# A rotary half swap done by VectorE products that write to other partitions, in place of SBUF-to-SBUF DMAs

## The chip, the cores and the metric

The kernel runs on one core of a Trainium2 chip. Its engines run their own instruction queues side by side and meet through semaphores: TensorE (PE in the profile; its weight loads are PEld), VectorE (DVE), ScalarE (ACT), GpSimd (POOL) and SyncE (SP). DMAs are issued from the queues of SP, ACT and POOL. The metric is the time of one execution on the device in microseconds, as the median of several runs.

## What is computed

The reference is a decoder trunk with two layers on 512 tokens of width 1024. Each layer adds the output of three token mixers that share one input projection (MLA attention with 4 heads, gated linear attention "GLA" with 4 heads, retention with 4 heads), and then the output of a convolutional gated MLP. The change concerns the rotary embedding, which the MLA queries, the one MLA key shared by all heads, and the retention queries and keys go through:

```python
def apply_rope(x, cos, sin):
    half = x.shape[-1] // 2
    c = cos[None, :, None, :].astype(x.dtype)
    s = sin[None, :, None, :].astype(x.dtype)
    x1, x2 = x[..., :half], x[..., half:]
    return jnp.concatenate([x1 * c - x2 * s, x2 * c + x1 * s], axis=-1)
...
q_nope, q_rope = q[..., :MLA_NOPE], apply_rope(q[..., MLA_NOPE:], cos, sin)
k_r = apply_rope(k_rope[:, :, None, :], cos, sin)[:, :, 0, :]
...
qh = apply_rope(q.reshape(B, S, RET_HEADS, RET_DK), cos, sin)
kh = apply_rope(k.reshape(B, S, RET_HEADS, RET_DK), cos, sin) * (RET_DK ** -0.5)
```

## The kernel before

Activations are kept with features on the 128 partitions and the 512 tokens along the free dimension. So the two halves of a rotary vector are two blocks of partitions: for the MLA key rows 0 to 31 and 32 to 63, for a pair of MLA query heads the same twice on 128 rows, for retention rows 0 to 63 and 64 to 127 (its weight columns are packed in that order).

Each large product is made of three matmuls (`mm3`): both operands are split into a high and a low part of type fp32r by `halves` or `split` (a cast and a subtraction), and high times high, high times low and low times high are summed in PSUM. Weights arrive by SP as `raw` (three buffers), are split into `whi` and `wlo`, and in the mixers the low part is finished by an accumulating DMA on POOL's queue. All accumulation tiles share eight PSUM banks, under the tags `g` (projections), `s` (scores, transposes) and `o` (outputs of attention).

Nothing is issued as it is written. A `Recorder` collects every instruction with its reads and writes, and `schedule` plans the whole program by list scheduling with its own costs and due times; `issue` then emits that order, in which each engine works strictly. In the planner's costs a DMA from ACT takes 0.1 us to issue, then its bytes at 200 KB per us and 2.0 us (`DMA_ISSUE`, `DMA_RATE`, `DMA_LATENCY`, lines 251 to 253). An instruction with more than one form (`copy`, `scale`) goes to the engine, ACT or DVE, that the planner finds free; `tt` has the one form, on DVE. Since all are emitted by one line of `issue`, the profile shows that line (L491) for almost everything, and rows are told apart by tile names: `z0` and the results of `scaled` are `t` or `w`, the rotary tables lie in `const_rope`, `qe` and `big` belong to the scores of GLA and retention.

One layer's mixer runs in this order of the program: projection `t0` (which holds the MLA key `z0` and the gate's input), `gq0`, `gk0`, the gate of GLA (`gla_gate`: a small matmul, three ScalarE functions, a running sum by four scans), `rq0` and `rk0` with their rotary, `gla_scores` (transposes of the decayed key `kh` early on TensorE, then seven levels with masks), `ret_scores`, the values, latents and gates, the MLA key's rotary `kz`, the linear outputs, the MLA up-projections with the rotary of two query pairs, four heads of `mla_head` (scores, mask, row maximum, exponent, transposes, product with the values), and the output projection, which is accumulated in halves: the part over the linear mixers can run early and fills TensorE between the heads' first blocks. Then comes the MLP (`ffn`).

A rotary in the kernel before: ACT's queue issues one DMA for each half block (two for the key and for retention, four for a query pair), each of which copies a half of `z` to the other half's rows in `zs`; DVE multiplies `z` by the cosine, then `zs` by the signed sine, and adds. The key's result is copied to rows 64 to 127 by one more DMA, and split on 128 rows. That is 15 DMAs a layer.

Of the kernel before, what the change touches and what calls it, by code (L numbers as in the profile page):

```python
# [18 lines left out]
F32 = mybir.dt.float32  # L19
F32R = mybir.dt.float32r  # L20
I32 = mybir.dt.int32
AF = mybir.ActivationFunctionType
ALU = mybir.AluOpType
# [3 lines left out]
S = 512  # L27
# [103 lines left out]
def constants():  # L131

    first, rope, rest = Stream(), Stream(), Stream()
    i = np.arange(P)
    first.add("one", np.ones((P, 1)))
    first.add("hm", (i[:, None] // 32 == np.arange(H)[None, :]))
    first.add("ident", np.eye(P))
    first.add("ones", np.ones((P, P)))

    first.add("bias", np.where(i[None, :] <= i[:, None], 0.0, MASK_BIAS))  # L140

    t = np.arange(S, dtype=np.float32)
    for name, dim, half in (("m", 64, 32), ("r", 32, 64)):
        inv = (np.float32(10000.0) ** (-(np.arange(0, dim, 2, dtype=np.float32) / np.float32(dim)))).astype(np.float32)
        ang = (t[None, :] * inv[:, None]).astype(np.float32).astype(np.float64)
        f = i % (dim // 2)
        sign = np.where(i % (2 * half) < half, -1.0, 1.0)
        rope.add("cos" + name, np.cos(ang)[f])
        rope.add("sin" + name, np.sin(ang)[f] * sign[:, None])
    gam = 1.0 - 2.0 ** (-5.0 - np.arange(H))  # L150
    diff = i[None, :] - i[:, None]
    dt = np.stack([np.where(diff >= 0, g ** np.maximum(diff, 0), 0.0) for g in gam], axis=1)
    rest.add("rdec", dt.reshape(P, H * P))
    gp = gam[RET_ROWS // 32]
    rest.add("qdec", gp[:, None] ** (i[None, :] + 1.0))
    rest.add("kdec", gp[:, None] ** (P - 1.0 - i[None, :]))
    rest.add("cdec", (gp ** P)[:, None])
    rest.add("bd", (i[:, None] // 32 == np.arange(256)[None, :] // 64))
    rest.add("bdr", (RET_ROWS[:, None] // 32 == np.arange(256)[None, :] // 64))
    rest.add("hmr", (RET_ROWS[:, None] // 32 == np.arange(H)[None, :]))  # L160
    for s in LEVELS:
        half = s // 2
        m = np.arange(64) // half
        rest.add(f"lm{s}", (i[:, None] >= m[None, :] * s) & (i[:, None] < m[None, :] * s + half))
    return {"first": first, "rope": rope, "rest": rest}


# [336 lines left out]
class Builder:  # L504
# [208 lines left out]
    def rope(self, z, half, rows, name, out):  # L713

        nc = self.nc
        zs, t1 = self.w(), self.w()
        for p in range(0, rows, 2 * half):
            nc.scalar.dma_start(out=zs[p:p + half], in_=z[p + half:p + 2 * half], bytes_=half * S * 4)
            nc.scalar.dma_start(out=zs[p + half:p + 2 * half], in_=z[p:p + half], bytes_=half * S * 4)
        self.tt(t1[:rows], z[:rows], self.c("cos" + name)[:rows], ALU.mult)  # L720
        self.tt(zs[:rows], zs[:rows], self.c("sin" + name)[:rows], ALU.mult)
        self.tt(out[:rows], zs[:rows], t1[:rows], ALU.add)
        return out

# [40 lines left out]
    def mix(self):  # L765
        nc = self.nc
# [24 lines left out]
        for name, sc in (("rq0", 1.0), ("rk0", DK_SCALE)):  # L791
            z = self.w()
# [38 lines left out]


        kz = self.rope(z0, 32, 64, "m", self.w())
        nc.scalar.dma_start(out=kz[64:128], in_=kz[0:64], bytes_=64 * S * 4)
        kr = self.halves(kz)

        sg = self.big(NB)
        for n, ps in enumerate(tokens("g")):
# [27 lines left out]
        for u, kinds in enumerate((("n", 0, "r", 0), ("n", 1, "n", 2), ("r", 1, "n", 3))):  # L866
            wt = self.wload(f"uq{u}")
            for j in range(2):
                kind, i = kinds[2 * j:2 * j + 2]
                ps = self.ps("g")  # L870
                self.gemm(ps, wt, j * 384, cq)
                z = self.w()
# [3 lines left out]
                else:  # L876
                    z = self.rope(z, 32, P, "m", self.w())
                    for h, (own, other) in enumerate(((slice(0, 64), slice(64, P)), (slice(64, P), slice(0, 64)))):
                        x = qr[2 * i + h] = self.t(F32R)
# [333 lines left out]
```

## Time and profile before

| | |
|---|---|
| median of 3 runs | 1230.01 us (1228.95 to 1232.84) |
| the profiled execution | 1230.06 us, of it 1228.1 us from first to last instruction |
| busy, share of the span | PE 97%, PEld 81%, DVE 70%, ACT 29%, POOL 4% |
| mean granted TensorE clock | 0.989 of full |

"Busy" of PE is the time in which at least one matmul is under way; matmuls overlap, and one of 512 columns starts about every 0.23 us at full clock. Rows of the timeline give the start and length of an instruction (or of several merged ones, with their count), and in brackets how long the engine stood idle before it and what released it. In the stages by time, the two mixers are 0 to 217.6 us and 617.3 to 819.4 us, and the MLPs follow them.

### The profile page before, as it was taken

The numbers are of one execution on the slowest core, as the hardware profiler recorded it, in microseconds if no ns is written. First come the engines' busy times: TensorE is split into PE (matmuls) and PEld (weight loads), VectorE is DVE, ScalarE is ACT, GpSimd is POOL, SyncE is SP. The second block draws the span as 40 slices with busy tenths as digits, with TensorE's granted clock in tenths as the row PEclk, the third lists the DMA queues.
The fourth block names the chain that finished last, engine by engine and source line by source line (L and its number), as shares of the span: only waits on it lengthen the run. The fifth ranks groups of instructions, "written<-read, shape, count | busy, mean of one in ns | idle before, by whom it ended". The sixth has DMA issues, their size and how long they took to land.

```text
span 1228.1 us, 14686 instructions
## 1 busy us (share of the span) xinstructions
PE 1188.4 (97%) x5700; PEld 993.4 (81%) x5700; DVE 865.0 (70%) x1461; ACT 360.8 (29%) x610; POOL 51.7 (4%) x63
## 2 busy tenths in 40 slices
PE   7899989999999999999998999899999999999996
PEld 5687878888888888888886788788888888888896
DVE  7699788677654666467758988776766557654775
ACT  5354636331110111012334556442311002100232
POOL 1011110100000000000011111000000000000000
PEclk9899999999999999999998999999999999999999
DMA  8765561733332333332486654617332333333322
GB/s 280 180 144 135 137 144 38 154 121 89 101 103 87 102 100 90 103 96 72 112 194 155 152 133 104 150 26 184 99 103 87 103 97 92 103 94 95 100 72 70
DMA packets 43174, 141.24 MB, mean 115 GB/s; under 512 B 4960, under 2 KB 7392, under 8 KB 42976
## 3 DMA queue, kind: packets, MB, share of 16 engines
q1 hardware_dynamic: 32848, 107.53, 28.7%
q0 software_dynamic: 8496, 30.15, 13.3%
q10 hardware_dynamic: 1760, 2.62, 0.8%
q8 instruction: 45, 0.74, 0.3%
q14 instruction: 25, 0.20, 0.0%
HBM read 105.42 MB, written 2.10 MB: 88 GB/s over the span
## 4 chain that ended last, share of the span: by engine, by line
PE 84%; DVE 8%; DMA 4%; ACT 1%; issue 1%; ACTq 1%; SPq 0%; DVEq 0%
PE g L491 57%; PE s L491 24%; DVE w L491 3%; DMA w<-w 3%; PE o L491 3%; DVE qe L491 2%; DVE big L491 1%; DVE t L491 1%; DMA w<-t 1%; ACTq L491 1%; DMA X<-x_in 0%; ACT w L491 0%; ACT whi L491 0%; SPq L491 0%; DVE sm L491 0%
## 5 line engine op out<-in xcount | busy, mean ns | idle before, releaser
L491 PE MATMUL g<-t,whi 128*128 128x512 f32 x2088 | 650.7, 392 | 6.5 <-ACT whi L491 6.2
L491 PEld LDWEIGHTS g<-t,whi 128*128 128x128 f32 x2088 | 391.7, 189 | 87.8 <-ACT whi L491 6.9
L491 PE MATMUL g<-t,wlo 128*128 128x512 f32 x1044 | 408.5, 392 | 0.0
L491 DVE CAST whi<-raw 128x1024 fp32r<-128x1024 f32 (+2 forms) x146 | 99.8, 684 | 236.3 <-PE g L491 130.4
L491 PEld LDWEIGHTS g<-t,wlo 128*128 128x128 f32 x1044 | 197.0, 189 | 40.2 <-DVE wlo L491 0.5
L491 PE MATMUL s<-t,whi 128*128 128x512 f32 x608 | 187.1, 389 | 0.0
L491 DVE TENSOR_TENSOR wlo<-raw,whi 128x1024 fp32r<-128x1024 f32 (+2 forms) x133 | 157.6, 1185 | 2.1 <-ACT whi L491 2.1
L491 ACT ACTIVATE w<-w,par 128x512 f32<-128x512 f32 x44 | 36.0, 817 | 371.1 <-DVE w L491 371.0
L491 PEld LDWEIGHTS s<-t,whi 128*128 128x128 f32 x608 | 114.2, 188 | 23.6
L491 PE MATMUL s<-t,wlo 128*128 128x512 f32 x304 | 118.3, 389 | 0.0
L491 PE MATMUL g<-whi,t 128*128 128x512 f32 x288 | 94.7, 404 | 0.0
L491 POOL DMA_DIRECT2D wlo<-raw x59 | 51.5, 873 | 790.2 <-ACT wlo L491 629.8
L491 PE MATMUL s<-t 128*128 128x256 f32 (+2 forms) x484 | 73.3, 305 | 6.1 <-DVE t L491 6.1
L491 PEld LDWEIGHTS s<-t 128*128 128x128 f32 x484 | 64.9, 195 | 8.5 <-DVE t L491 6.9
L491 ACT ACTIVATE w<-w 128x512 f32<-128x512 f32 (+1 forms) x82 | 44.6, 558 | 88.5 <-DVE w L491 88.0
L491 DVE SCALAR_TENSOR_TENSOR w<-w,par 128x511 f32<-128x511 f32 x88 | 65.8, 748 | 1.4
L491 PEld LDWEIGHTS s<-t,wlo 128*128 128x128 f32 x304 | 57.1, 188 | 11.9
L491 PEld LDWEIGHTS g<-whi,t 128*128 128x128 f32 x288 | 55.7, 195 | 11.8 <-issue 0.8
L491 ACT CAST whi<-raw 128x1024 fp32r<-128x1024 f32 (+2 forms) x46 | 46.0, 1000 | 63.7 <-PE g L491 39.1
L491 ACT CAST t<-w 128x512 fp32r<-128x512 f32 (+1 forms) x51 | 31.6, 620 | 104.9 <-DVE w L491 96.6
L491 ACT ACTIVATE wlo<-whi 128x1024 fp32r<-128x1024 f32 (+1 forms) x45 | 46.8, 1041 | 44.5 <-PE g L491 21.7
L491 PE MATMUL g<-wlo,t 128*128 128x512 f32 x144 | 58.1, 404 | 0.0
(120 smaller groups left out, 1038.5 us busy)
## 6 DMA issues: line engine op xcount, KB each, us to landing
raw<-w_l SPq DMA_DIRECT2D x174, 512.0 KB, 3.5
wlo<-raw POOLq DMA_DIRECT2D x53, 512.0 KB, 4.9
raw<-w_l SPq DMA_DIRECT2D x22, 384.0 KB, 3.2
wlo<-raw POOLq DMA_DIRECT2D x6, 384.0 KB, 4.0
X<-x_in SPq DMA_DIRECT2D x8, 256.0 KB, 6.0
out<-w SPq DMA_DIRECT2D x8, 256.0 KB, 2.4
w<-w ACTq DMA_DIRECT2D x10, 128.0 KB, 3.6
raw<-w_l SPq DMA_DIRECT2D x4, 256.0 KB, 4.6
```

Source lines behind the costliest of these rows:

```text
L491: getattr(getattr(nc, eng), method)(**kw)
```

## The change

Each half is multiplied by the sine on the rows where it lies, and the product is written to the other half's rows of `zs`. The table's sign therefore goes with the row that is read, so the signs of the two halves are exchanged. The DMAs and the one sine product on all rows go. The key is split on its 64 rows, and its two parts are copied to rows 64 to 127 by ScalarE or VectorE.

```diff
-        sign = np.where(i % (2 * half) < half, -1.0, 1.0)
+        sign = np.where(i % (2 * half) < half, 1.0, -1.0)
...
         zs, t1 = self.w(), self.w()
+        sin = self.c("sin" + name)
         for p in range(0, rows, 2 * half):
-            nc.scalar.dma_start(out=zs[p:p + half], in_=z[p + half:p + 2 * half], bytes_=half * S * 4)
-            nc.scalar.dma_start(out=zs[p + half:p + 2 * half], in_=z[p:p + half], bytes_=half * S * 4)
+            lower, upper = slice(p, p + half), slice(p + half, p + 2 * half)
+            self.tt(zs[lower], z[upper], sin[upper], ALU.mult)
+            self.tt(zs[upper], z[lower], sin[lower], ALU.mult)
         self.tt(t1[:rows], z[:rows], self.c("cos" + name)[:rows], ALU.mult)
-        self.tt(zs[:rows], zs[:rows], self.c("sin" + name)[:rows], ALU.mult)
         self.tt(out[:rows], zs[:rows], t1[:rows], ALU.add)
...
         kz = self.rope(z0, 32, 64, "m", self.w())
-        nc.scalar.dma_start(out=kz[64:128], in_=kz[0:64], bytes_=64 * S * 4)
-        kr = self.halves(kz)
+        kr = self.t(F32R), self.t(F32R)
+        self.copy(kr[0][0:64], kz[0:64])
+        self.tt(kr[1][0:64], kz[0:64], kr[0][0:64].bitcast(F32), ALU.subtract)
+        for x in kr:
+            self.copy(x[64:128], x[0:64].bitcast(F32))
```

The planner makes a new order of the whole program. Its emitting line is now L492. SP's and POOL's queues keep their sequence of operations; those of PE, DVE and ACT change.

The first place is VectorE's order at the start of the first layer's mixer, where the key's rotary (`const_rope`, 64 rows) stands among the instructions of the gate (`w<-s,par`, the subtraction behind it, four scans `t<-const_first,w`). Before:

```order
L491 TENSOR_TENSOR w_384<-t_364,const_rope_163 64x512
L491 TENSOR_TENSOR w_388<-t_370,t_379 128x512
L491 TENSOR_SCALAR w_391<-s_374,par0_135 128x512
L491 TENSOR_TENSOR w_376<-w_376,const_rope_163 64x512
L491 TENSOR_TENSOR w_391<-w_391,w_386 128x512
L491 TENSOR_TENSOR w_407<-w_376,w_384 64x512
L491 SCALAR_TENSOR_TENSOR t_412<-const_first_159,w_391 128x128 x4
```

And of the change, at the same place:

```order
L492 TENSOR_TENSOR w_381<-t_364,const_rope_163 32x512
L492 TENSOR_TENSOR w_385<-t_370,t_376 128x512
L492 TENSOR_SCALAR w_388<-s_374,par0_135 128x512
L492 TENSOR_TENSOR w_381<-t_364,const_rope_163 32x512
L492 TENSOR_TENSOR w_388<-w_388,w_383 128x512
L492 TENSOR_TENSOR w_404<-t_364,const_rope_163 64x512
L492 SCALAR_TENSOR_TENSOR t_409<-const_first_159,w_388 128x128 x4
L492 TENSOR_TENSOR w_419<-w_381,w_404 64x512
```

Before, the product with the swapped rows `w_376`, which a DMA writes, stands ahead of the gate's subtraction and scans; now no instruction here reads what a DMA of ACT wrote, and one more product stands there.

The second place is VectorE's order from the scans' end to `kh`, the product (`t_379` or `t_376` is the key of GLA) that TensorE's next transposes read. Before, from the projection of `rq0` on:

```order
L491 TENSOR_TENSOR w_452<-g_353,rs_356 128x512
L491 TENSOR_TENSOR w_461<-w_452,const_rope_163 128x512
L491 CAST whi_469<-raw_397 128x1024
L491 TENSOR_SCALAR wlo_474<-whi_469 128x1024
L491 TENSOR_TENSOR w_459<-w_459,const_rope_163 128x512
L491 CAST whi_486<-raw_421 128x1024
L491 TENSOR_TENSOR t_490<-w_459,w_461 128x512
L491 SCALAR_TENSOR_TENSOR w_497<-g_358,rs_356 128x512
L491 TENSOR_TENSOR w_505<-t_370,w_426 128x512
L491 TENSOR_TENSOR w_513<-w_497,const_rope_163 128x512
L491 TENSOR_TENSOR w_520<-t_379,w_424 128x512
```

And of the change:

```order
L492 TENSOR_TENSOR w_453<-g_353,rs_356 128x512
L492 TENSOR_TENSOR t_458<-w_433,t_446 128x512
L492 TENSOR_TENSOR w_463<-w_453,const_rope_163 64x512 x2
L492 TENSOR_TENSOR w_473<-w_453,const_rope_163 128x512
L492 TENSOR_TENSOR t_480<-w_419,t_428 64x512
L492 TENSOR_TENSOR t_485<-w_463,w_473 128x512
L492 TENSOR_TENSOR w_491<-t_376,w_426 128x512
```

The three weight conversions and the projection of `rk0` no longer stand ahead of `kh`, and the product of swapped rows is now two products on 64 rows.

The third place is VectorE's order in the attention, at the rotary of the first query pair (`z` is `w_1709` or `w_1707`, the added result `w_1760` or `w_1748`; the scores need `t<-w_1760` of 64 rows). Before:

```order
L491 SCALAR_TENSOR_TENSOR w_1709<-g_1689,rs_1273 128x512
L491 TENSOR_TENSOR w_1716<-w_1709,const_rope_163 128x512
L491 TENSOR_SCALAR wlo_1726<-whi_1711 128x1024
L491 SCALAR_TENSOR_TENSOR w_1732<-g_1706,rs_1273 128x512
L491 CAST t_1738<-w_1732 128x512
L491 TENSOR_TENSOR t_1744<-w_1732,t_1738 128x512
L491 TENSOR_TENSOR w_1719<-w_1719,const_rope_163 128x512
L491 SCALAR_TENSOR_TENSOR w_1755<-g_1729,rs_1273 128x512
L491 TENSOR_TENSOR w_1760<-w_1719,w_1716 128x512
L491 CAST t_1767<-w_1755 128x512
L491 CAST t_1771<-w_1760 64x512
L491 TENSOR_TENSOR t_1778<-w_1755,t_1767 128x512
```

And of the change:

```order
L492 SCALAR_TENSOR_TENSOR w_1707<-g_1687,rs_1260 128x512
L492 TENSOR_TENSOR w_1714<-w_1707,const_rope_163 32x512 x4
L492 TENSOR_TENSOR w_1734<-w_1707,const_rope_163 128x512
L492 SCALAR_TENSOR_TENSOR w_1740<-g_1704,rs_1260 128x512
L492 TENSOR_TENSOR w_1748<-w_1714,w_1734 128x512
L492 SCALAR_TENSOR_TENSOR w_1755<-g_1723,rs_1260 128x512
L492 CAST t_1761<-w_1748 64x512
L492 TENSOR_TENSOR t_1768<-w_1740,t_1752 128x512
L492 TENSOR_TENSOR t_1758<-w_1748,t_1758 64x512
L492 TENSOR_TENSOR t_1761<-w_1748,t_1761 64x512
L492 TENSOR_TENSOR t_1783<-w_1755,t_1774 128x512
L492 SCALAR_TENSOR_TENSOR w_1790<-g_1742,rs_1260 128x512
```

Four products on 32 rows take the place of the sine product, the weight conversion and two casts go to ScalarE, and the split of the rotated pair moves up. TensorE's order there has 18 matmuls of the output projection after the scores of the first query blocks, where it had 3 to 6.

## Rows read from the trace of the kernel before

**Rows 1.** The page's first part: busy us, share of the span and instructions by engine.
```profile
PE 1188.4 (97%) x5700; PEld 993.4 (81%) x5700; DVE 865.0 (70%) x1461; ACT 360.8 (29%) x610; POOL 51.7 (4%) x63
```
**Rows 2.** Busy time by stretch: length, then busy us (instructions) by engine, granted clock.
```profile
0.00:217.60 217.60, 198.96 (x1029) 165.58 (x1030) 180.13 (x370) 109.78 (x200) 20.66 (x27) 0.98 0.59 149
217.60:617.30 399.70, 399.70 (x1766) 330.99 (x1766) 258.43 (x351) 74.45 (x105) 6.89 (x8) 1.00 0.37 104
617.30:819.40 202.10, 190.68 (x1010) 160.94 (x1010) 164.80 (x344) 99.23 (x182) 19.86 (x23) 0.97 0.56 131
```
**Rows 3.** Timeline of TensorE: first matmuls, and its long waits in both mixers.
```profile
5.81 1.22 PE L491 MATMUL g<-t,whi 128*128 128x512 f32 x2 [5.81 <-ACT whi L491]
...
51.36 0.76 PE L491 MATMUL s<-const_first,w 128*128 128x128 f32 x3 [4.71 <-DVE w L491]
...
180.08 6.37 PE L491 MATMUL s<-t 128*128 128x512 f32 x27 [3.73 <-DVE t L491]
...
649.78 0.90 PE L491 MATMUL s<-const_first,w 128*128 128x128 f32 x3 [4.59 <-DVE w L491]
...
779.75 4.84 PE L491 MATMUL s<-t 128*128 128x512 f32 x27 [2.37 <-DVE t L491]
...
786.51 0.66 PE L491 MATMUL s<-const_first,w 128*128 128x128 f32 x4 [1.21 <-ACT w L491]
...
789.11 0.90 PE L491 MATMUL s<-const_first,w 128*128 128x128 f32 x3 [1.49 <-ACT w L491]
```
**Rows 4.** Timeline of VectorE: instructions that stood behind a swap DMA.
```profile
36.07 0.68 DVE L491 TENSOR_TENSOR w<-w,const_rope 64x512 f32<-64x512 f32 x1 [4.56 <-DMA w<-t]
...
42.29 0.43 DVE L491 CAST t<-w 128x512 fp32r<-128x512 f32 x1 [1.64 <-DMA w<-w]
...
47.00 0.69 DVE L491 TENSOR_TENSOR w<-w,const_rope 128x512 f32<-128x512 f32 x1 [0.90 <-DMA w<-w]
...
176.16 0.69 DVE L491 TENSOR_TENSOR w<-w,const_rope 128x512 f32<-128x512 f32 x1 [4.69 <-DMA w<-w]
...
629.62 0.68 DVE L491 TENSOR_TENSOR w<-w,const_rope 64x512 f32<-64x512 f32 x1 [3.22 <-DMA w<-t]
...
635.90 0.69 DVE L491 TENSOR_TENSOR t<-w,t 128x512 fp32r<-128x512 f32 x1 [3.67 <-ACT t L491]
...
646.50 0.69 DVE L491 TENSOR_TENSOR w<-w,const_rope 128x512 f32<-128x512 f32 x1 [2.29 <-DMA w<-w]
```
**Rows 5.** Timeline of ScalarE: a cast behind the key's copy, and four swap issues.
```profile
168.27 2.66 ACTq L491 DMA_DIRECT2D w<-w  x4
...
635.24 0.62 ACT L491 CAST t<-w 128x512 fp32r<-128x512 f32 x1 [8.30 <-DMA w<-w]
```
**Rows 6.** Busy time of 10 us stretches after the four stops; the clock stands third from last.
```profile
50.00:60.00 10.00, 8.64 (x33) 7.06 (x34) 7.53 (x12) 4.65 (x7) 1.45 (x2) 0.83 0.93 211
180.00:190.00 10.00, 9.79 (x51) 8.78 (x52) 8.78 (x19) 4.91 (x9) 0.86 (x1) 0.83 0.54 135
...
650.00:660.00 10.00, 10.00 (x35) 8.07 (x34) 7.73 (x12) 4.33 (x7) 0.86 (x1) 0.71 0.76 184
...
790.00:800.00 10.00, 10.00 (x74) 9.61 (x73) 7.78 (x28) 6.34 (x21) 0.00 (x0) 0.89 0.19 54
```
**Rows 7.** Timeline of VectorE: two operations on the same rows, two that shift rows.
```profile
36.68 1.28 DVE L491 TENSOR_TENSOR w<-w 128x512 f32<-128x512 f32 x2
...
187.87 1.40 DVE L491 TENSOR_TENSOR t<-w,t 64x512 fp32r<-64x512 f32 x2
```
**Rows 8.** Timeline of VectorE: the scaling that makes the first query pair's `z`, by layer.
```profile
167.55 0.69 DVE L491 SCALAR_TENSOR_TENSOR w<-g,rs 128x512 f32<-128x512 f32 x1
...
768.58 0.69 DVE L491 SCALAR_TENSOR_TENSOR w<-g,rs 128x512 f32<-128x512 f32 x1
```
**Rows 9.** Busy time of the stretch of GLA's and retention's scores, first layer.
```profile
57.30:126.80 69.50, 66.97 (x333) 54.46 (x332) 68.47 (x122) 37.13 (x60) 8.49 (x10) 1.00 0.63 146
```

## The prediction

> **What bounds the kernel now.** The page's first part comes first: TensorE is under way 97% of the span, VectorE 70% [rows 1]. So what can be won is what TensorE loses, and the stretches show where: in the MLP behind the first mixer it has no idle time in 399.70 us; in the mixers it stands idle 217.60 − 198.96 = 18.6 us and 202.10 − 190.68 = 11.4 us [rows 2]. The timeline of TensorE puts names to these 30.0 us [rows 3]. 5.81 us are the wait for the first weights. In each layer there are two places where it stops: ahead of the transposes of `kh` (4.71 and 4.59 us, released by VectorE's `w`), and inside the first attention scores (3.73 us; in the second layer 2.37, and then 1.21 and 1.49 ahead of transposes that wait for an exponent). That is 4.71 + 4.59 + 3.73 + 2.37 + 1.21 + 1.49 = 18.1 us; the other 6.1 us are many small waits.
>
> Then the timeline of VectorE, since it releases most of these. Just ahead of each stop it stood idle itself, for a rotary product whose swapped rows had not landed: 4.56, 1.64 and 0.90 us ahead of the first layer's `kh`, 4.69 ahead of its scores, 3.22, 3.67 and 2.29 ahead of the second layer's `kh` [rows 4]. The 3.67 came by way of ScalarE, which stood 8.30 us on a cast of the key behind the key's copy, with the gate's functions queued behind it; it also spends 2.66 us on issuing the four swaps of a query pair [rows 5]. Each queue is strictly in order, so what stands behind the sine product waits too although it doesn't need it: the gate's subtraction and scans, the splits of MLA's queries and keys.
>
> The stops also cost clock. [...] Taken as 10 us × (1 − clock), that is 1.7 + 1.7 + 2.9 + 1.1 = 7.4 us.
>
> **What the change takes away and adds.** *Removed:* 15 DMAs a layer with their landing times and ACT's issue time, and the five sine products on all rows, one for each rotary.
>
> *Added on VectorE:* 2 products for the key, 2 each for retention's query and key, 4 each for two query pairs, 14 instead of 5. A product on 32 rows isn't in the trace. Two operations on the same rows take 1.28 us, the second starting 1.28 − 0.68 = 0.60 behind the first; two subtractions on 64 rows that write to the other 64 take 1.40, so 1.40 − 0.69 = 0.71 [rows 7]. I take 0.71, since the new products shift rows as those do; the low bound is 0.60, and the high one 0.91 above it (below, the third rival) is where the change would lose. 14 × 0.71 − 5 × 0.60 = 6.9 us more on VectorE per layer. The key's extra copies on 64 rows go to whichever of ScalarE and VectorE is free; the queue position of the last of them has over 100 us until the attention reads it.
>
> [...]
>
> *At `kh`, both layers.* VectorE loses 4.56 + 1.64 + 0.90 = 7.1 us of waits in the first layer, and gains ahead of `kh` one product for the key and one for `rq0`, at most 2 × 0.71 + 4 × 0.11 (for what follows a shifted one) = 1.9 us; the new order also puts three weight conversions and `rk0`'s projection behind `kh`. So `kh` comes at least 7.1 − 1.9 = 5.2 us earlier, more than TensorE's 4.71. In the second layer 3.22 + 3.67 + 2.29 = 9.2, less 1.9 and two casts of 0.43 [rows 4] for the key: 6.4 us, more than 4.59. Both stops go, and the lower clock behind them. What is late next is the first level's `qe`: the planner asks for it 8 matmuls earlier than before in the first layer and some 12 earlier in the second. I leave 0.3 and 0.8 us for that.
>
> From there the scores run for 69.5 us in which VectorE is busy 68.47 and TensorE 66.97 [rows 9]. The rotaries are over by then; the order has the same count of products, masks and casts between the first and the last mask. So this stretch should keep its length and move forward whole.
>
> *In the attention, both layers.* The first pair's `z` is ready at 167.55 + 0.69 = 168.24 [rows 8]. The new order then has four products and the cosine (5 × 0.71), a projection (0.60), the sum (0.71), a projection (0.60), a cast (0.43 as in [rows 4]), a split (0.60) and the split that the scores read (0.71): 7.2 us, so 175.4. TensorE's stop began at 180.08 − 3.73 = 176.35 [rows 3]: the operand is there 0.9 us earlier. In the second layer 768.58 + 0.69 + 7.2 = 776.5 [rows 8] against 779.75 − 2.37 = 777.4. The stops of 3.73 and 2.37 go. Those of 1.21 and 1.49 had the exponents behind ScalarE's issues and the second pair's swap; both go. In their place, the first mask now stands behind the second pair's four products. TensorE has 18 matmuls of the output projection as cover there, at about 0.23 us each 4.1 us; without that cover the mask's delay of some 2.8 us would show in each layer. I leave 0.5 us per layer.
>
> **The sum.** 18.1 us of stops + 7.4 us of clock − (0.3 + 0.8 + 0.5 + 0.5) = 23.4 us. The profiled execution took 1230.06 us, like the median of 1230.01: 1230.06 − 23.4 = 1206.7 us.
>
> **The rivals.**
>
> *First: the attention gives half back.* The early use of the output projection as cover leaves fewer matmuls later, and the 4 × 0.71 us of the second pair ahead of the first mask come through. Against it: later blocks had no such cover before either. Price: 2.8 us of stop and 1.7 us of clock [rows 6] in each layer, 9.0 us: 1215.7 us.
>
> *Second: VectorE's end is the end anyway.* With 68.47 of 69.5 us busy [rows 9], a delay of that stretch by the added products of the first two rotaries, or another split of casts, goes straight into TensorE's waits. If `kh` comes only as much earlier as is needed but the levels behind it slip by the 6.9 us of added work per layer, 1206.7 + 13.8 = 1220.5 us. Against it: half of these products stand in the attention, not here.
>
> *Third: slower, because products that shift between groups of 32 rows are dear.* 28 of them stand in the two layers, nearly all on the path as worked out above. It decides from 25.5 ÷ 28 = 0.9 us above the 0.71 that I took, so 1.6 us each; at 2.0 us, 1206.7 + 28 × 1.3 = 1243 us. For it: no row has 32 rows. Against it: the pair on 64 rows costs only 0.11 more than an ordinary one [rows 7].
>
> [...]
>
> *Fourth: the transfers were hidden, and TensorE waits elsewhere.* The new order shifts the work, but the same time results: 1230 us. For it: the planner has covered 97% of the span [rows 1]. Against it: the stops are released by exactly the queues that stood on the swaps.
>
> **How the numbers follow.** Forecast as worked out, 1199 to 1212 us: 0.70. First rival 0.13, second 0.09, fourth 0.04, third 0.04. If also all the 6.1 us of small waits went and nothing were left of the stops, it would be 1230.06 − 25.5 − 6.1 = 1198.5; the low end is 1199. The high end takes in the first rival, up to 1218; the second, third and fourth, 0.17, lie outside. No change means within 0.3%, 3.7 us, which is about what a measurement of this kernel can tell. Faster: 0.70 + 0.13 + 0.09 = 0.92; same 0.04; slower 0.04.
>
> **What would show it.** Right: ACT's queue has no DMAs; VectorE has no idle time released by `w` DMAs; TensorE's waits ahead of `kh`'s transposes and in the first scores are under 1 us each; the granted clock stays at 1.00 in the four stretches; both mixers are 11 to 13 us shorter, and the MLPs as long as before. The 32-row products start 0.71 us apart. Wrong: a new wait of TensorE over 2 us ahead of the attention's first transposes (first rival), small waits at each level of the scores that add up (second), products of over 1.5 us (third). What would break the forecast altogether is another planner's order that starves TensorE of weights in the values' projection, where it now arrives some 6 us sooner.

## The result, and the profile after

The changed kernel takes 1215.42 us (median of 4 runs, 1214.21 to 1215.69); the kernel before takes 1230.88 beside it (4 runs, 1228.95 to 1232.84). The ratio is 0.9872, 95% interval 0.9854 to 0.9891. That is a gain of 15.5 us where 23.4 was forecast. The sign held. The time lies outside the 1199 to 1212 us that had a chance of 0.70, and within the range only because its high end, 1218, took in the first rival. The profiled execution took 1214.21 us, with a span of 1212.4.

The page's first part, to be read beside [rows 1]:

```profile
PE 1182.8 (98%) x5700; PEld 987.9 (81%) x5700; DVE 870.5 (72%) x1468; ACT 371.5 (31%) x625; POOL 51.9 (4%) x63
```

VectorE has 5.5 us more to do and yet the program ends sooner. The change adds 22 instructions, 18 products and four copies of the key's parts; in the new order VectorE runs 7 more than before and ScalarE 15 more (10.7 us), since casts went there. The timeline of TensorE in the mixers, its waits that answer to [rows 3]:

```profile
42.72 0.55 PE L492 MATMUL s<-const_first,w 128*128 128x128 f32 x3 [0.50 <-DVE w L492]
...
179.19 0.89 PE L492 MATMUL s<-const_first,w 128*128 128x128 f32 x5 [1.17 <-ACT w L492]
...
218.23 0.80 PE L492 MATMUL g<-t,wlo 128*128 128x512 f32 x1 [2.61 <-DMA wlo<-raw]
...
643.91 0.39 PE L492 MATMUL s<-qe,w 128*128 128x256 f32 x1 [0.25 <-DVE qe L492]
...
773.20 0.89 PE L492 MATMUL s<-const_first,w 128*128 128x128 f32 x5 [1.17 <-ACT w L492]
...
812.25 0.79 PE L492 MATMUL g<-t,wlo 128*128 128x512 f32 x1 [2.57 <-DMA wlo<-raw]
```

The waits of 4.71 and 4.59 us ahead of `kh` are 0.50 us and less, and those of 3.73 and 2.37 inside the first scores are gone; 1.17 us stand ahead of the first transposes. But two rows are new, at 218.23 and 812.25: in the output projection TensorE waits for a DMA that finishes the low part of weights. They cost clock as well, as the windows show (the stretches of [rows 6] first, then those of the new waits; the clock stands third from last):

```profile
50.00:60.00 10.00, 9.69 (x52) 8.03 (x51) 10.00 (x20) 4.02 (x6) 1.72 (x2) 1.00 0.62 120
180.00:190.00 10.00, 10.00 (x81) 9.53 (x80) 6.49 (x23) 6.63 (x20) 0.00 (x0) 1.00 0.11 42
650.00:660.00 10.00, 9.96 (x55) 8.25 (x55) 9.97 (x19) 5.65 (x7) 1.72 (x2) 1.00 0.60 146
790.00:800.00 10.00, 10.00 (x70) 9.08 (x69) 6.97 (x23) 5.86 (x18) 0.00 (x0) 1.00 0.01 2
...
210.00:240.00 30.00, 27.38 (x113) 21.89 (x112) 17.53 (x27) 9.96 (x14) 4.63 (x5) 0.94 0.74 169
800.00:830.00 30.00, 27.42 (x116) 21.83 (x115) 16.98 (x30) 9.29 (x13) 4.32 (x5) 0.94 0.63 139
```

The old losses of clock are repaid. The new ones are 30 × 0.06 = 1.8 us in each layer. With the idle time, 2.62 and 2.58 us, that makes 4.4 us a layer, 8.8 in all. By this estimate the places that the forecast spoke of would have given 15.5 + 8.8 = 24.3 us.

What happens there is read from the chain of waits of the changed kernel around the first new wait (start, length, what):

```profile
208.46 2.10 PE g L492 x9
...
210.58 0.69 DVE whi L492
...
211.79 0.68 DVE X L492
212.47 0.62 DVE wlo L492
...
213.60 4.58 DMA wlo<-raw
218.18 0.04 issue
218.23 3.88 PE g L492 x9
```

`whi` and `wlo` have three buffers each. They hold `wo0`, `wo1` and `wo2`, the weights of the first three output blocks, until the last head is done. Only when the matmuls on `wo0` end, near 210.5, can `wo3` be converted: a cast, two residual additions that stand ahead of the scale in VectorE's queue (1.2 us), the scale, POOL's issue and an accumulating DMA of 4.58 us, 7.6 us up to 218.18. What TensorE can do meanwhile, its cover, is the rest of `wo1` and `wo2` and the first matmuls on the high part of `wo3`. TensorE's timeline shows where that cover ends. The kernel before, where the cast of `wo3` starts at 219.71:

```profile
219.71 0.69 DVE L491 CAST whi<-raw 128x1024 fp32r<-128x1024 f32 x1 [0.61 <-PE g L491]
...
226.53 1.07 PE L491 MATMUL g<-t,whi 128*128 128x512 f32 x4
227.44 0.39 PE L491 MATMUL g<-t,wlo 128*128 128x512 f32 x1
```

The changed kernel, where it starts at 210.58 (the low part is first used at 218.23, in the row above):

```profile
210.58 0.69 DVE L492 CAST whi<-raw 128x1024 fp32r<-128x1024 f32 x1 [0.61 <-PE g L492]
...
213.80 1.82 PE L492 MATMUL g<-t,whi 128*128 128x512 f32 x6
```

Before, TensorE uses the low part 227.44 − 219.71 = 7.7 us after the cast's start, and doesn't wait. After, it is out of other work at 213.80 + 1.82 = 215.62, 5.0 us after the cast's start, and 7.6 − 5.0 = 2.6 us is the wait. The missing matmuls were run in the first scores: from 171.9 to 178.1 us the changed kernel runs 20 matmuls that write `g`, and 38 from there to the end of `wo0`; the kernel before runs 3 up to 187 us, and 40 from there.

How much a whole mixer gained shows at VectorE's eight residual additions `X<-X,g`, one behind each output block. Before, and then after, in the two layers:

```profile
L491 DVE TENSOR_TENSOR X<-X,g x8: 679/681/682, 220.3 to 254.3; 128x512 f32<-128x512 f32 x8
...
L491 DVE TENSOR_TENSOR X<-X,g x8: 679/681/682, 822.1 to 856.1; 128x512 f32<-128x512 f32 x8
...
L492 DVE TENSOR_TENSOR X<-X,g x8: 679/681/689, 211.2 to 246.4; 128x512 f32<-128x512 f32 x8
...
L492 DVE TENSOR_TENSOR X<-X,g x8: 680/681/686, 805.2 to 840.3; 128x512 f32<-128x512 f32 x8
```

By the last addition each mixer is 7.9 us shorter (254.3 against 246.4, and 601.8 against 593.9 from there to 856.1 and 840.3), and what follows the second of them is as long as before (372.0 and 372.1 us).

### The profile page after: what moved, and what is told of

It is laid out like the page before. It is cut to its first block, busy times and chain, and to the rows that moved or that the text cites. A ratio compares the mean times of both kernels' runs of the same rounds, so it can differ in the third digit from the quotient of the medians.

```text
span 1212.4 us, 14622 instructions
## 1 busy us (share of the span) xinstructions
PE 1182.8 (98%) x5700; PEld 987.9 (81%) x5700; DVE 870.5 (72%) x1468; ACT 371.5 (31%) x625; POOL 51.9 (4%) x63
## 3 DMA queue, kind: packets, MB, share of 16 engines
q0 software_dynamic: 8496, 30.15, 13.5%
## 4 chain that ended last, share of the span: by engine, by line
PE 79%; DVE 18%; DMA 1%; issue 1%; ACT 1%; SPq 0%; DVEq 0%; POOLq 0%; ACTq 0%
PE g L492 53%; PE s L492 24%; DVE w L492 8%; DVE t L492 3%; DVE qe L492 3%; PE o L492 2%; DVE big L492 2%; DMA wlo<-raw 1%; DVE sm L492 1%; DMA X<-x_in 1%; ACT w L492 0%; SPq L492 0%; DVE st L492 0%; DVE whi L492 0%; DVE X L492 0%
## 5 line engine op out<-in xcount | busy, mean ns | idle before, releaser
L492 PE MATMUL g<-t,whi 128*128 128x512 f32 x2088 | 652.3, 392 | 7.0 <-ACT whi L492 6.4
L492 PEld LDWEIGHTS g<-t,whi 128*128 128x128 f32 x2088 | 392.1, 189 | 89.3 <-ACT whi L492 8.0
L492 PE MATMUL g<-t,wlo 128*128 128x512 f32 x1044 | 408.6, 392 | 5.2 <-DMA wlo<-raw 5.2
L492 DVE CAST whi<-raw 128x1024 fp32r<-128x1024 f32 (+2 forms) x143 | 97.5, 682 | 226.7 <-PE g L492 120.7
L492 PEld LDWEIGHTS g<-t,wlo 128*128 128x128 f32 x1044 | 197.1, 189 | 45.9 <-DMA wlo<-raw 6.1
L492 PE MATMUL s<-t,whi 128*128 128x512 f32 x608 | 187.1, 389 | 0.0
L492 DVE TENSOR_TENSOR wlo<-raw,whi 128x1024 fp32r<-128x1024 f32 (+2 forms) x133 | 157.6, 1185 | 2.2 <-ACT whi L492 2.2
L492 ACT ACTIVATE w<-w,par 128x512 f32<-128x512 f32 x44 | 36.0, 817 | 371.1 <-DVE w L492 371.0
L492 PEld LDWEIGHTS s<-t,whi 128*128 128x128 f32 x608 | 114.2, 188 | 23.7
L492 PE MATMUL s<-t,wlo 128*128 128x512 f32 x304 | 118.3, 389 | 0.0
L492 PE MATMUL g<-whi,t 128*128 128x512 f32 x288 | 92.1, 392 | 0.0
L492 POOL DMA_DIRECT2D wlo<-raw x59 | 51.7, 880 | 774.7 <-ACT wlo L492 540.4
L492 ACT ACTIVATE w<-w 128x512 f32<-128x512 f32 (+1 forms) x82 | 44.7, 558 | 90.3 <-DVE w L492 89.8
L492 PE MATMUL s<-t 128*128 128x256 f32 (+2 forms) x484 | 71.8, 301 | 0.0
L492 DVE SCALAR_TENSOR_TENSOR w<-w,par 128x511 f32<-128x511 f32 x88 | 65.8, 748 | 1.4
L492 PEld LDWEIGHTS s<-t,wlo 128*128 128x128 f32 x304 | 57.1, 188 | 11.8
L492 ACT CAST whi<-raw 128x1024 fp32r<-128x1024 f32 (+2 forms) x49 | 49.3, 1005 | 55.9 <-PE g L492 47.1
L492 PEld LDWEIGHTS s<-t 128*128 128x128 f32 x484 | 63.6, 191 | 1.5
L492 ACT CAST t<-w 128x512 fp32r<-128x512 f32 (+1 forms) x57 | 35.3, 620 | 93.9 <-DVE w L492 93.9
L492 PEld LDWEIGHTS g<-whi,t 128*128 128x128 f32 x288 | 53.6, 188 | 10.9 <-issue 0.8
L492 PE MATMUL g<-wlo,t 128*128 128x512 f32 x144 | 56.5, 392 | 0.0
L492 DVE TENSOR_TENSOR w<-w,rs 128x512 f32<-128x512 f32 x44 | 30.5, 692 | 33.2 <-ACT w L492 33.2
```

The costliest lines, as they stand in the source:

```text
L492: getattr(getattr(nc, eng), method)(**kw)
```

## The experiments

The questions were: whether the new wait is all that is missing; which of the two places pays; whether it is the swap's landing that costs or the order around it; and what the added products cost. The kernel before was run beside each group, with medians of 1230.9, 1230.5 and 1230.0 us. Every ratio is to it.

**1. The new wait taken away.** In the changed kernel the low part of `wo3` alone is made by a subtraction on VectorE, without a DMA.

```diff
-            if parts > 1 or name[:2] in ("ua", "ub", "dn") or (self.layer == 0 and name == "gk0"):
+            if parts > 1 or name[:2] in ("ua", "ub", "dn") or name == "wo3" or (self.layer == 0 and name == "gk0"):
```

> Changed kernel, but the low part of the fourth output projection's weights (wo3) is made by one VectorE subtraction instead of the scale and the accumulating DMA of POOL. Theory (the missing 8 us went into the stops of 2.61 and 2.57 us at the end of each mixer, where TensorE waits for the DMA that finishes wo3's low part, and into the clock behind them, 0.91 and 0.92, then 0.83): both stops fall under 1 us, the granted clock stays near 1.00 there, and the time is 1215.4 less 7 to 9 us, about 1207. Rival (the attention gives back in many places what it gained, and the end is only where it shows): another wait of 2 to 3 us takes their place, for VectorE or for wo4's weights, and the time stays at 1213 to 1217.

Measured: 1205.34 us (1204.41 to 1205.63), ratio 0.9794 (0.978 to 0.9807). The windows of the two stretches:

```profile
210.00:240.00 30.00, 30.00 (x134) 24.85 (x133) 21.84 (x33) 10.79 (x15) 3.44 (x4) 1.00 0.75 183
800.00:830.00 30.00, 30.00 (x134) 24.83 (x133) 21.56 (x33) 10.78 (x15) 3.44 (x4) 1.00 0.78 193
```

No idle time, full clock, and nothing in its place: the theory holds, and a little more than 8.8 us comes back (10.1), so the time is 1.1 us below the band that was expected. The last additions of the two layers stand at 241.5 and 830.7 us, so the mixers are 12.8 and 12.6 us shorter than before, as the prediction said (11 to 13).

**2. The same edit in the kernel before.**

> Kernel before with the same edit for wo3 alone. Theory (in the kernel before a whole output projection of 24 matmuls lies ahead of wo3, so that its DMA is hidden): no change within 0.3%, 1227 to 1234. Rival (POOL's DMA costs something in either kernel): 4 us or more faster, 1226 or less.

Measured: 1230.59 us, ratio 0.9994 (0.9984 to 1.0005). No cost of `wo3`'s DMA shows there. The change made it a bound.

**3. One place at a time.** In one kernel the query pairs swap by DMAs and the rest by products; in the other it is the reverse. The table keeps its new signs, so the DMA form subtracts.

```diff
+        dma = (half, rows) == (32, P)
         for p in range(0, rows, 2 * half):
             lower, upper = slice(p, p + half), slice(p + half, p + 2 * half)
-            self.tt(zs[lower], z[upper], sin[upper], ALU.mult)
-            self.tt(zs[upper], z[lower], sin[lower], ALU.mult)
+            for to, src in ((lower, upper), (upper, lower)):
+                if dma:
+                    nc.scalar.dma_start(out=zs[to], in_=z[src], bytes_=half * S * 4)
+                else:
+                    self.tt(zs[to], z[src], sin[src], ALU.mult)
         self.tt(t1[:rows], z[:rows], self.c("cos" + name)[:rows], ALU.mult)
-        self.tt(out[:rows], zs[:rows], t1[:rows], ALU.add)
+        if dma:
+            self.tt(zs[:rows], zs[:rows], sin[:rows], ALU.mult)
+        self.tt(out[:rows], t1[:rows], zs[:rows], ALU.subtract if dma else ALU.add)
```

The second kernel has `!=` in the first line. The first one:

> Changed kernel, but the two query pairs of each layer swap by DMAs from ScalarE's queue as before; key and retention by products. Theory (the places ahead of kh gave about 8 us in each layer together with the clock, 7.9 us by the start of the linear outputs in the first layer, and the attention's gain was taken back at the end of the mixer): stops of 2 to 4 us in the first attention scores come back, those for wo3's weights at the end go, and the time stays within 5 us of the changed kernel's, 1212 to 1220. Rival (the attention is worth its 4 to 5 us per layer, and the stop at the end comes from the earlier part of the mixer being faster): the stops at the end stay at over 2 us and the time is 8 to 10 us above the changed kernel's, 1223 to 1226.

Measured: 1216.3 us, ratio 0.9888 (0.9872 to 0.9904), a gain of 14.6 us. TensorE's timeline has the waits of the attention again, and none for `wo3`:

```profile
172.21 6.37 PE L492 MATMUL s<-t 128*128 128x512 f32 x27 [2.16 <-DVE t L492]
...
767.43 0.73 PE L492 MATMUL s<-t 128*128 128x512 f32 x2 [2.00 <-DVE t L492]
...
777.51 0.90 PE L492 MATMUL s<-const_first,w 128*128 128x128 f32 x3 [2.19 <-ACT w L492]
```

The second kernel:

> Changed kernel, but key and retention swap by DMAs as before, and only the query pairs by products. Theory (the attention's gain is given back at the end of the mixer): the stops ahead of kh stay at 4 to 5 us each, those in the first scores go, the ones for wo3's weights at the end appear with 2 to 3 us, and the time is 1226 to 1231. Rival (the attention gives 4 to 5 us per layer that is kept): 1220 to 1223, with no stop over 1 us at the end of the mixers.

Measured: 1227.38 us, ratio 0.9975 (0.9962 to 0.9987), a gain of 3.6 us. The waits for `wo3` are there, 2.58 and 2.57 us at 228.34 and 825.67. The waits of the first part stay, though in another shape than expected: 1.79, 1.24 and 4.02 us in the first layer, 3.03 in the second. So the theory holds in both in the main: the places at `kh` pay almost all of what the change gains, and products for the queries bring the wait at the end of the mixer, which takes back most of what they win. With that wait gone, they add 1216.3 − 1205.3 = 11.0 us.

**4. The landing or the order.** The kernel before keeps all its DMAs. Only the planner's figure for the landing of ScalarE's DMAs is raised from 2.0 us.

```diff
-                op.end = begin + op.size / DMA_RATE[e] + DMA_LATENCY
+                op.end = begin + op.size / DMA_RATE[e] + (5.0 if e == "ACT" else DMA_LATENCY)
```

> Kernel before, DMAs and all, but the planner counts 5.0 us instead of 2.0 us for the landing of a DMA from ScalarE's queue (and bytes as before), so that it puts other work ahead of what reads the swapped rows. Theory (it is the landing itself, late for work that TensorE needs next, that costs): the stops ahead of kh and in the first scores stay at 2 us or more in sum for each place, and the time stays at 1224 or more. Rival (what costs is that the planner places the sine product too early, so that work which doesn't need the swap stands behind it): most of the stops go and the time is 1210 to 1220, near the changed kernel's.

Measured: 1209.42 us, ratio 0.9823 (0.9807 to 0.9838). The theory falls, and the rival holds, its band passed by 0.6 us: with every swap still a DMA the kernel is faster than the changed one. Two more values followed, 3.5 and 8.0 us, since one good order could be luck.

> Kernel before with 3.5 us instead of 2.0 us as the planner's landing time of ScalarE's DMAs (5.0 gave 1209.4). Theory (the planner's figure is too short, so the sine products stand too early in VectorE's order and hold up work that doesn't need them; the more of the true landing is counted, the fewer stops are left): between the two, 1208 to 1222, with the stops ahead of kh smaller than 4.7 and 4.6 us. Rival (5.0 happened on a good order): 1225 or more.

> The same with 8.0 us, more than any swap needed in the trace. Theory: the swaps wait for nothing, but what reads their result comes later than it must, above all in the first attention scores; ahead of kh no stops, 1207 to 1215 in all. Rival (5.0 happened on a good order): 1220 or more.

Measured: 1217.54 us at 3.5 (ratio 0.9898, 0.988 to 0.9916) and 1213.53 us at 8.0 (0.9867, 0.9849 to 0.9885). Both lie in the bands of their theories, so 5.0 was not luck. In the groups by line, the rotary products' row gives VectorE's idle time ahead of them and how much of it ended with a swap's DMA. The kernel before (planned at 2.0 us):

```profile
L491 DVE TENSOR_TENSOR w<-w,const_rope 128x512 f32<-128x512 f32 (+1 forms) x18 | 12.4, 690 | 25.5 <-DMA w<-w 17.6 <-DMA w<-t 7.8
```

Planned at 3.5:

```profile
L491 DVE TENSOR_TENSOR w<-w,const_rope 128x512 f32<-128x512 f32 (+1 forms) x18 | 12.4, 689 | 16.9 <-DMA w<-w 11.3 <-DMA w<-t 5.4
```

At 5.0:

```profile
L491 DVE TENSOR_TENSOR w<-w,const_rope 128x512 f32<-128x512 f32 (+1 forms) x18 | 12.1, 686 | 7.0 <-DMA w<-t 4.5 <-DMA w<-w 2.5
```

At 8.0:

```profile
L491 DVE TENSOR_TENSOR w<-w,const_rope 128x512 f32<-128x512 f32 (+1 forms) x18 | 12.2, 685 | 0.2
```

25.5, 16.9, 7.0, 0.2 us, with the same 18 instructions, ten of which read rows that a DMA swapped. What the swaps cost is where the planner put their readers in a strictly ordered queue. At 5.0 the waits ahead of `kh` are gone in both layers, and only 2.47 and 2.13 us in the first scores are left. Although each figure gives a new order of the whole program, these places make up nearly all of the gain: of the 18.1 us of stops that the prediction lists 4.6 are left, 13.5 less, and the mean granted clock is 0.994 instead of 0.989, worth about 6 us of the span by this estimate, where the profiled runs differ by 20.3. At 8.0 those fall too, to 0.95 in the second layer and none over 0.5 in the first, and the wait for `wo3` appears, as it does with the products. So what is lost at 8.0 shows at the end of the mixers, and not, as its theory had it, in the first scores:

```profile
220.23 0.65 PE L491 MATMUL g<-t,wlo 128*128 128x512 f32 x1 [1.68 <-DMA wlo<-raw]
...
812.40 0.50 PE L491 MATMUL g<-t,wlo 128*128 128x512 f32 x1 [1.73 <-DMA wlo<-raw]
```

That wait therefore doesn't belong to the products. It came in each order that leaves `wo3` to the DMA and has no wait over 1.2 us in the first scores of the attention: the changed kernel, the queries alone, this one, and one more below. It came in none of those that wait longer there: the kernel before, queries by DMA, and the planner's 3.5 and 5.0.

**5. The price of the products.** On the kernel of experiment 1, each shifted product is issued twice.

```diff
-            self.tt(zs[lower], z[upper], sin[upper], ALU.mult)
-            self.tt(zs[upper], z[lower], sin[lower], ALU.mult)
+            for _ in range(2):
+                self.tt(zs[lower], z[upper], sin[upper], ALU.mult)
+                self.tt(zs[upper], z[lower], sin[lower], ALU.mult)
```

> The version with wo3's low part by subtraction (1205.3 us), with every shifted product issued twice, the second writing the same values again: 14 more products a layer, 9.9 us more work on VectorE in each layer at 0.71 us. Theory (most of the added products lie beside TensorE's work): less than half of it shows, 1205 + 3 to 9 us, and most of that in the first scores of the attention, where the stop of 1.17 us grows to 2 to 4 us. Rival (VectorE's end is the end, and each product goes into the time): 1205 + 16 to 20 us, 1221 to 1225.

Measured: 1225.6 us, ratio 0.9957 (0.9945 to 0.9969), 20.3 us more than the 1205.3. The theory falls; the rival holds, its band passed by 0.6 us. In its residual additions, layer by layer:

```profile
L492 DVE TENSOR_TENSOR X<-X,g x8: 680/682/689, 220.2 to 254.3; 128x512 f32<-128x512 f32 x8
...
L492 DVE TENSOR_TENSOR X<-X,g x8: 679/680/687, 821.0 to 851.8; 128x512 f32<-128x512 f32 x8
```

Experiment 1 has 211.1 to 241.5 and 800.3 to 830.7. The first addition comes 9.1 us later in the first layer, and in the second 7.9 us later, counted from the last of the first (821.0 − 254.3 against 800.3 − 241.5): 17 of the 28 × 0.70 = 19.6 us added. Most of the rest is a wait of 2.51 us in the first layer for another block's weights, and its clock. So in this one run, past the point where the products fit into the time that VectorE lost before, each one counts nearly in full. It does not follow that removing some would gain:

**6. A mixture, and three more runs on the attention and the end of the mixer.** Key and retention by DMAs that are planned at 5.0 us, the query pairs by products, `wo3` by subtraction (the edits of experiments 1 and 4, and that of the second kernel of experiment 3, together):

> Key and retention swap by DMAs that the planner counts at 5.0 us, the query pairs by products, and wo3's low part by subtraction. Theory (ahead of kh a swap that is planned rightly costs no more than the products, and in the attention, where nothing else is at hand, the products win about 2 us a layer and its clock): 1202 to 1206, no worse than the 1205.3 of products alone. Rival (the products are what makes kh early): 1207 to 1212, with stops ahead of kh or in the scores behind it.

Measured: 1206.72 us (1205.29 to 1209.08), ratio 0.9812 (0.9792 to 0.9832). The median lies between the two bands. The intervals of this kernel and of experiment 1 overlap, and in the first 60 us of the first layer, past `kh`, no wait but one of 0.83 us at the gate and those for the first weights is over 0.6 us. Swaps planned rightly and products are worth the same there, within what these runs can tell. The kernel before with both a better figure and `wo3` by subtraction was not run, so whether the products for the queries are worth more than that is open.

The changed kernel with 4.0 instead of 2.0 us as the planner's landing time of POOL's DMAs:

> The changed kernel, with 4.0 us instead of 2.0 us as the planner's landing time of POOL's DMAs. Theory (the stop at the end of the mixers is no misjudged landing: wo3's weights can't start before wo0's are used up, and the matmuls that could cover them have been spent in the heads): stops of 2 us or more for wo3's low part stay, and the time stays at 1211 or more. Rival (the planner would keep the cover if it counted the DMA longer): the stops fall under 1 us and the time is 1205 to 1209.

Measured: 1216.64 us, ratio 0.9892 (0.9874 to 0.9909), and the waits are longer:

```profile
222.06 0.50 PE L492 MATMUL g<-t,wlo 128*128 128x512 f32 x1 [3.12 <-DMA wlo<-raw]
...
816.14 0.50 PE L492 MATMUL g<-t,wlo 128*128 128x512 f32 x1 [3.10 <-DMA wlo<-raw]
```

The theory holds: a longer figure cured the swaps, but this wait is not a misjudged landing. The planner's own sum for this DMA, 524,288 bytes at 187,000 per us and 2.0 us, is 4.8 us, and the trace has 4.58. That fits a list scheduler, which takes work when it is ready and saves none as cover; that itself was not tried.

The changed kernel with the low parts of all eight output blocks by subtraction (`"wo"` added to the tuple of experiment 1, instead of `wo3`):

> The changed kernel with the low parts of all eight output projections' weights by VectorE subtraction. Theory (only wo3's DMA was late): the time is that of wo3 alone, 1204 to 1207. Rival (VectorE has no room for 8 subtractions of about 1.2 us instead of scales of half of that at the end of each mixer, or the other DMAs cost something too): 1208 or more, or 1203 or less.

Measured: 1215.36 us, ratio 0.9877 (0.9861 to 0.9893), 10.0 us worse than `wo3` alone. There is no wait at the end of the mixers, but the first attention starts like this on TensorE:

```profile
172.49 1.52 PE L492 MATMUL g<-t,whi 128*128 128x512 f32 x6
177.47 0.66 PE L492 MATMUL s<-const_first,w 128*128 128x128 f32 x4 [3.46 <-ACT w L492]
```

The early cover is 6 matmuls here, all with a high part. The low part of `wo0` is a subtraction that VectorE hasn't done by then; its first one for these weights starts at 180.40. The wait for the first exponent, 1.17 us in the changed kernel, becomes 3.46 in each layer. With another wait of 0.73 us behind it and a granted clock of 0.96 and 0.87 in the stretches of 10 us from 170 and 180, that is 2.3 + 0.7 + 1.7 = 4.7 us in the first layer, about half of the 10.0. The rival's first half holds, by way of the cover rather than of the end.

Last, on the kernel of experiment 1, the second query pair's rotary is written behind the first head:

```diff
         for h in range(H):
+            if h == 1:
+                pair(1, second)
             ys[h] = self.mla_head(h, qn[h], qr[h], kn[h], kr, vm)
```

(`pair` holds the rotary and the split of one pair, and `second` is its `z`.)

> The version with wo3's low part by subtraction, with the second query pair's rotary written after the first head instead of ahead of it, so that the first mask no longer stands behind its products. Theory (the stop of 1.17 us ahead of the first transposes in each attention is the mask's delay behind those products): it goes in both layers, and the time is 1205.3 less 1.5 to 3 us, about 1203. Rival (the first exponent is what the transposes wait for, whatever VectorE does): the stop stays at about 1.2 us, or another of that length comes ahead of the third head's scores, and the time stays at 1204.5 to 1206.5.

Measured: 1206.33 us (1205.65 to 1207.69), ratio 0.9804 (0.9789 to 0.9818). The wait falls to 0.52 us in both layers, nearly as the theory said, and the time doesn't follow: it lies in the rival's band. In the 40 us from 170 on TensorE is busy 39.04 us against 38.83 in experiment 1, so of the 0.65 us by which this wait fell only 0.21 shows there; the rest is back in a wait of 0.44 us ahead of later scores, at 180.74. Of the 1.2 us by which the profiled run is longer than that of experiment 1, 0.95 are there at `kh` already (43.56 against 42.61), ahead of what the edit touches. The theory was right about the cause of the wait and wrong about its worth.

## Why the prediction was right, and where it was off

*The places at `kh`.* Right, and near in size. By the prediction's terms they are 4.71 + 1.7 − 0.3 and 4.59 + 2.9 − 0.8, 12.8 us together; experiment 3, which has only these, gives 14.6. The other signs came out too: no DMA on ScalarE's queue, no idle time of VectorE that a swap ended [rows 4], full clock in the four stretches of [rows 6]. The prediction's 7.4 us of clock are worked out from the clocks of [rows 6]; after the change each of these stretches has 1.00. The scores behind moved forward whole, as [rows 9] let one expect: from the first level's `qe` to that of a later level, for which TensorE waits 0.94 us, it is 39.7 us (52.23 to 91.90), and 40.1 before (61.74 to 101.88).

*The places in the attention.* Right by themselves. The terms are 3.73 + 1.7 − 0.5 and 2.37 + 1.21 + 1.49 + 1.1 − 0.5, 10.6 us; the difference of experiments 3 and 1 is 11.0. The waits of 1.17 us ahead of the first transposes are twice the 0.5 that was left for them, and the last run of experiment 6 shows that they cost less than their length.

*The step that failed* is one term that is missing from the sum. The prediction saw that the output projection's matmuls are used early as cover in the attention. Under the first rival it named the price, fewer matmuls later, and dismissed it with "later blocks had no such cover before either". That looked at the heads' blocks. It did not look at the projection's own weights, for which the same matmuls were the cover: 7.7 us before, against a conversion of 7.6. After, 5.0 us are left, and 10.1 us were lost in the two layers (experiments 1 and 2). It was easy to miss, since the stretch that it takes for the MLP [rows 2] starts at 217.60 us, with most of the output projection in it (additions from 220.3 to 254.3), and has no idle time in the kernel before. The sentence on what would break the forecast had the kind right, an order that starves TensorE of weights, and the place wrong: the output projection, not the values' projection. The first rival's time, 1215.7, is close to what was measured, and fewer matmuls later is what happened; but its price was taken from the second pair's products ahead of the mask, which is not what cost. That the two times agree is luck.

*The cause, as the prediction put it,* was half right. "What stands behind the sine product waits too although it doesn't need it" is the cause; experiment 4 shows it. That the DMAs themselves had to go does not follow: with another figure in the planner, the kernel with the same 15 swaps a layer is 21 us faster. The fourth rival, transfers that are hidden anyway, was wrong of the kernel before, and nearly true of it with a better order.

*The price of the products* was right. Five in a row on VectorE, four of them on 32 rows and then the cosine, and the groups by shape:

```profile
170.19 3.48 DVE L492 TENSOR_TENSOR w<-w,const_rope 32x512 f32<-32x512 f32 x5
```

```profile
L492 DVE TENSOR_TENSOR w<-w,const_rope 32x512 f32<-32x512 f32 x16 | 10.9, 683 | 0.3
L492 DVE TENSOR_TENSOR w<-w,const_rope 128x512 f32<-128x512 f32 x8 | 5.5, 692 | 0.1
```

(3.48 − 0.68) ÷ 4 = 0.70 us from start to start against the 0.71 taken, and 683 ns for one on 32 rows against 692 on 128. That rules out the third rival, which needed 1.6 us. The operation itself is not longer on 32 rows; what it costs more is the start of the next, 0.70 us behind it, where two operations on the same rows start 0.60 apart [rows 7].

*The second rival's mechanism* did not decide: the scores' stretch did not grow (39.7 us against 40.1), and VectorE had 25.5 us of waits to lose. Experiment 5 shows how near it was: a second set of the same products costs 20.3 us.

## What to carry to other kernels

An in-order queue turns a late operand into a wait for everything behind it (here VectorE stood 4.69 us for one late swap [rows 4]), so before replacing a transfer try where its reader stands (here one number in the planner, 21 us). When a change makes TensorE use spare matmuls early, list every later transfer that these matmuls had covered, with its length and with what cover is left. Put the fix only where the wait is: here one block's low part gave 10 us, and the same edit on all eight gave nothing.

## What the runs showed of the hardware that was not expected

The times to landing of small swaps between rows scatter widely, and a product waits for the last of its swaps. In the kernel before, the median from issue to landing is 2.1 us for 16 of 64 KB, 3.6 for 10 of 128 KB, and 5.9 for 4 more of 64 KB, where the planner has 2.0 us and 0.3 or 0.7 for the bytes; the shortest took 2.0 and the longest 7.3. Of the four swaps of the first query pair, issued from 168.27 on, the one that took longest needed 5.5 us and the median is 2.0; their product started at 176.16 [rows 4]. ScalarE's queue was also held by the issues, a median of 0.58 us for each of those four, where the planner has 0.1. Planned at 5.0 us, the same groups took 4.4, 3.3 and 6.1. The time depended on when they ran more than on their size. What they shared the DMA engines with at those times was not tried.

A wait of 2.6 us on TensorE came with 1.8 us of lost clock behind it in each mixer (0.94 over 30 us, and 0.50 of full from 219 to 221 us and from 813 to 815). The waits of 1.17 us left the clock at 1.00 in the 10 us stretches from 170 and 180.
